# A planner's price for a three-pass matmul: 2.2 columns a nanosecond in place of 2.4

## The chip, the cores and the metric

The kernel runs on one core of one Trainium2 chip. The metric is the device time of one execution in microseconds (us), taken over several runs; a profile of one execution goes with it. The engines are TensorE (PE in the rows, PEld for its weight loads), VectorE (DVE), ScalarE (ACT), GpSimd (POOL) and SyncE (SP), which issues the DMAs.

## The reference

One inference step through two layers of a hybrid backbone, for 128 context tokens and 512 latent tokens that share the weights (float32 throughout). Cut to what is computed in each layer:

```python
mod = SiLU(cond) @ w_mod[l] + b_mod[l]          # shift1, scale1, gate1, shift2, scale2, gate2
h = rms_norm(x) * (1 + scale1) + shift1
proj = h @ w_in[l]     # q | k | v | z | x,B,C of the scan | dt | gate_attn | gate_ssd
attn = softmax(rope(norm(q)) @ rope(norm(k)).T * s) @ v      # 8 query heads, 2 key heads of 128
ssd = norm(ssd_scan(SiLU(dwconv3(x, B, C)), dt, both directions) * SiLU(z))   # chunks of 128
merged = sigmoid(gate_attn) * (attn @ w_attn_o) + sigmoid(gate_ssd) * (ssd @ w_ssd_o)
x = x + gate1 * (merged @ w_out)
h = rms_norm(x) * (1 + scale2) + shift2
u, g = dwconv3(h @ w_up)
x = x + gate2 * ((SiLU(g) * u) @ w_down)
```

Widths: model 1024, inner width of the scan 2048, feed-forward 2816. Keys, values and final scan states of the context tokens are outputs too.

## The kernel before

All 640 tokens, five tiles of 128, pass through each weight once. A float32 product is made of three passes: both operands are split into a high part, which the reduced float32 type `F32R` holds, and a low part, and high x high, low x high and high x low are accumulated in PSUM (`tok_major`, `feat_half`). ScalarE casts a weight block of 128 x 2048 to its high part `wh`, VectorE subtracts to get `wl`. Products with tokens on the partitions have 512 columns and write tiles `pf`; those with features on the partitions (`feat_half`: the convolved inputs of the scan and the up-projection) come in two halves of 386 and 256 columns, also `pf`. Scores of the attention have 320 columns (`pp`), its products with values 512 (`p`), as have the scan's (`p`, `pp`). Transposes and the scan's inner products are plain float32.

Nothing in the program's text is in the order of execution. While the layers are written down, each operation is only recorded, with its engine, a cost in nanoseconds from `_cost`, the earlier operations that it depends on, the buffers that it touches, and a class: `f` for the main stream of projections, `d` for attention and scan, `m` for the modulation of the next layer. Then `issue` plays the whole program through as a list scheduler. It keeps a clock for each of five lanes (TensorE, ScalarE, VectorE, GpSimd, and the one DMA queue), takes again and again the lane that can start something first, and starts on it the ready operation that ranks first:

```python
RANK = {
    "pe": {"m": 0, "d": 1, "f": 2}, "act": {"f": 0, "d": 1, "m": 2}, "dve": {"f": 0, "d": 1, "m": 2},
...
heapq.heappush(avail[e], (self.RANK[e][ops[i][5]], i))
```

So on TensorE an attention or scan operation goes in front of the main stream as soon as the plan says that its operands are there. An operation is ready when its predecessors end, plus a latency from a table `LAT` (160 ns from ScalarE or VectorE to TensorE, 197 ns back), and when a buffer of its kind is free. At the end all operations are issued in the order of their planned starts:

```python
for i in sorted(range(n), key=lambda k: (start[k], k)):
    ops[i][1]()
```

The chip sees only this order: each engine runs its instructions in it and waits where an operand isn't there. VectorE's prices in `_cost` are 70 + 1.04 ns a column (and 60 for each scalar operand), 0.53 ns a column for plain scalings out of SBUF; ScalarE's 52 or 95 + 0.832 ns a column and 93 for each scalar operand. The planner doubles TensorE's prices while it takes its clock for the lower level.

Every operation is recorded by one helper, so all of them have line 178 in the rows, and tiles tell them apart.

Of the kernel before, what the change touches and what calls it, by code (L numbers as in the profile page):

```python
# [79 lines left out]
class Flow:  # L80
# [99 lines left out]
    @staticmethod  # L180
    def _cost(lane, fn, outs, ins, kw):
        def free(ap):
            n = 1
            for d in ap.shape[1:]:
                n *= d
            return n

        n = free(outs[0])
        if lane == "dma":
            return free(outs[0]) * outs[0].shape[0] * 4 / 360.0  # L190
        if lane == "pe":
            if fn == "transpose":
                return 110.0
            if ins[0].dtype == F32R:
                return max(n, 256) / 2.4 + 2 if n > 128 else 213.0
            return max(4 * n / 2.4, 213.0)
        psum = any(a.space == PSUM for a in ins)
        scalars = sum(isinstance(a, bass.AP) for k, a in kw.items() if k in ("scale", "bias", "accum_out"))
        if lane == "act":
            return (52 if psum else 95) + 0.832 * n + 93 * scalars  # L200
        if lane == "pool":
            return 165.0 * n + 300 if ALU.pow in kw.values() else 160.0
        scalars = len(ins) - (2 if fn in ("scalar_tensor_tensor", "tensor_tensor") else 1)
        if fn == "tensor_reduce":
            return 70 + 1.04 * free(ins[0])
        if fn == "reciprocal":
            return 70 + 6.2 * n
        if fn in ("tensor_scalar", "tensor_copy", "memset"):
            return 66 + (1.04 if psum else 0.53) * n + 60 * scalars
        if fn == "scalar_tensor_tensor":  # L210
            return 70 + 1.04 * n + 60 * scalars
        return 70 + 1.04 * n
# [1372 lines left out]
```

## Time and profile before

| | |
|---|---|
| median of 3 runs | 2854.1 us (2854.01 to 2860.25) |
| profiled execution, its own time | 2856.14 us |
| its span in the trace | 2854.3 us |
| TensorE, weight loads | 2816.9 us (99%), 2455.4 us (86%) |
| VectorE, ScalarE, GpSimd | 2067.6 us (72%), 1291.3 us (45%), 90.3 us (3%) |
| data moved | 478.45 MB, 168 GB/s |

The span is the time from the first to the last instruction of the profiled execution. A row of a group gives the engine, the operation, out<-in by tile names, the shape, the count, and then the busy time in us with the mean of one in ns; records of matmuls overlap their neighbours, so a stream's pace is read from starts, not from durations.

### The profile page before, as it was taken

The page shows a single profiled execution, that of the slowest core. Times are in us where ns is not written, and L with a number is a line of the kernel's source. Part 1 is how long each engine was busy: PE and PEld are TensorE (multiplying, and loading weights), DVE is VectorE, ACT ScalarE, POOL GpSimd, SP SyncE. Part 2 cuts the span into 40 slices and gives each one's busy share as a digit, 9 for nine tenths or more (in the row PEclk, how much of TensorE's full clock was granted, in tenths as well). Part 3 has the DMA queues.
Part 4 walks back from the last instruction along what each step waited for, and adds up shares of the span by engine and source line. Part 5 has one row for each costly group of instructions (what it writes and reads, how often), then busy time and mean ns, then how long its engine had stood idle before and what let it go on. Part 6 is the DMA issues. An engine that isn't in the chain of part 4 may idle for free.

```text
span 2854.3 us, 41196 instructions
## 1 busy us (share of the span) xinstructions
PE 2816.9 (99%) x15620; PEld 2455.4 (86%) x15620; DVE 2067.6 (72%) x2851; ACT 1291.3 (45%) x2255; POOL 90.3 (3%) x408
## 2 busy tenths in 40 slices
PE   7999999999999999999999999999999999999999
PEld 4898997788788898998979989878887888989898
DVE  7878775987799599997677666598778456545554
ACT  6454544445353453442444645544454325524342
POOL 1100000000000000000011000000000000000000
PEclk9999999999999999999999999999999999999999
DMA  7344344676768546455352323457667654251523
GB/s 260 104 126 137 114 151 155 209 255 245 276 214 277 177 139 213 164 180 174 104 164 83 95 94 100 151 203 251 221 241 250 205 171 136 86 166 65 157 83 111
DMA packets 309679, 478.45 MB, mean 168 GB/s; under 512 B 19808, under 2 KB 139792, under 8 KB 304360
## 3 DMA queue, kind: packets, MB, share of 16 engines
q1 hardware_dynamic: 309480, 475.81, 49.8%
q8 instruction: 123, 2.02, 0.3%
q14 instruction: 76, 0.62, 0.1%
HBM read 384.08 MB, written 91.65 MB: 167 GB/s over the span
## 4 chain that ended last, share of the span: by engine, by line
PE 94%; DMA 3%; DVE 1%; ACT 1%; issue 0%; SPq 0%; DVEq 0%; ACTq 0%
PE pf L178 79%; PE p L178 10%; PE pp L178 3%; PE pq L178 1%; DMA slab<-in_w_mod_dram 0%; DVE tmp L178 0%; DVE wl L178 0%; DMA tmp<-in_state_ssd_dram 0%; DMA tmp<-sz 0%; DMA mw<-in_w_mod_dram 0%; DMA tmp<-in_x_prompt_dram 0%; DVE slab L178 0%; DMA tmp<-xs 0%; ACT tmp L178 0%; DMA slab<-row 0%
## 5 line engine op out<-in xcount | busy, mean ns | idle before, releaser
L178 PE MATMUL pf<-wh,slab 128*128 128x512 f32 x3920 | 1268.9, 400 | 6.5 <-DVE tmp L178 2.5
L178 PE MATMUL pf<-slab,wh 128*128 128x256 f32 (+1 forms) x4416 | 979.5, 311 | 3.3 <-DVE slab L178 1.9
L178 PEld LDWEIGHTS pf<-wh,slab 128*128 128x128 f32 x3920 | 733.3, 189 | 175.8 <-issue 7.6
L178 PE MATMUL pf<-wl,slab 128*128 128x512 f32 x1960 | 781.5, 399 | 0.2 <-DVE wl L178 0.2
L178 PEld LDWEIGHTS pf<-slab,wh 128*128 128x128 f32 x4416 | 741.1, 188 | 11.9 <-issue 5.5
L178 PE MATMUL pf<-slab,wl 128*128 128x256 f32 (+1 forms) x2208 | 684.5, 310 | 0.0
L178 DVE TENSOR_TENSOR wl<-wr,wh 128x2048 fp32r<-128x2048 f32 (+1 forms) x156 | 350.7, 2248 | 144.4 <-ACT wh L178 143.8
L178 PEld LDWEIGHTS pf<-wl,slab 128*128 128x128 f32 x1960 | 369.6, 189 | 87.1 <-issue 5.8
L178 ACT CAST wh<-wr 128x2048 fp32r<-128x2048 f32 (+1 forms) x156 | 293.0, 1879 | 319.9 <-PE pf L178 302.3
L178 PEld LDWEIGHTS pf<-slab,wl 128*128 128x128 f32 x2208 | 415.6, 188 | 3.1 <-issue 0.2
L178 DVE SCALAR_TENSOR_TENSOR tmp<-tmp,fw,tmp 128x642 f32<-128x642 f32 x176 | 155.5, 885 | 81.0 <-ACT tmp L178 67.0
L178 PE MATMUL p<-tmp,slab 128*128 128x64 f32 (+1 forms) x976 | 209.9, 336 | 1.4 <-DMA tmp<-xs 1.0
L178 ACT ACTIVATE tmp<-tmp 128x642 f32<-128x642 f32 (+2 forms) x176 | 120.9, 687 | 180.1 <-DVE tmp L178 142.3
L178 ACT ACTIVATE tmp<-pf,fw 128x386 f32<-128x386 f32 (+1 forms) x176 | 108.9, 619 | 175.9 <-PE pf L178 172.6
L178 DVE TENSOR_TENSOR tmp<-pf,tmp 128x512 f32<-128x512 f32 x100 | 68.3, 688 | 133.9 <-PE pf L178 133.4
L178 PEld LDWEIGHTS p<-tmp,slab 128*128 128x128 f32 x976 | 136.2, 190 | 17.3 <-ACT tmp L178 4.4
L178 ACT COPY tmp<-pf 128x256 f32<-128x256 f32 (+3 forms) x296 | 127.3, 431 | 43.9 <-PE pf L178 43.8
L178 DVE TENSOR_TENSOR slab<-tmp,slab 128x512 fp32r<-128x512 f32 (+4 forms) x182 | 109.0, 634 | 41.5 <-ACT slab L178 41.3
L178 DVE SCALAR_TENSOR_TENSOR macc<-tmp,cT,macc 128x512 f32<-128x512 f32 x196 | 137.8, 743 | 0.8 <-DMA tmp<-in_w_mod_dram 0.8
L178 DVE TENSOR_TENSOR tmp<-tmp,tmp 128x512 f32<-128x512 f32 (+3 forms) x190 | 133.6, 705 | 5.7 <-DMA tmp<-sz 3.0
L178 ACT ACTIVATE tmp<-pf 128x512 f32<-128x512 f32 (+1 forms) x110 | 63.5, 577 | 141.5 <-PE pf L178 133.6
L178 PEld LDWEIGHTS p<-cst,tmp 128*128 128x128 f32 (+2 forms) x750 | 91.7, 140 | 39.4 <-issue 13.1
(131 smaller groups left out, 2622.1 us busy)
## 6 DMA issues: line engine op xcount, KB each, us to landing
wr<-in_w_in_dram SPq DMA_DIRECT2D x60, 1024.0 KB
wr<-in_w_up_dram SPq DMA_DIRECT2D x44, 1024.0 KB
slab<-row SPq DMA_DIRECT2D x40, 1024.0 KB
tmp<-in_w_mod_dram SPq DMA_DIRECT2D x116, 256.0 KB
tmp<-xres SPq DMA_DIRECT2D x85, 256.0 KB
wr<-in_w_down_dram SPq DMA_DIRECT2D x20, 1024.0 KB
tmp<-xs SPq DMA_DIRECT2D x72, 256.0 KB
xres<-tmp SPq DMA_DIRECT2D x70, 256.0 KB
```

The costliest lines, as they stand in the source:

```text
L178: self.ops.append((lane, lambda: call(*args, **kw), self._cost(lane, fn, outs, ins, kw), deps, touched, self.cls))
```

## The change

One line of `_cost` changes: the planned duration of a three-pass product (operands of type `F32R`) of more than 128 columns. The old one is the columns, at least 256, at 2.4 a nanosecond, plus 2 ns; the new one is the same columns at 2.2 a nanosecond without the 2 ns. Shorter ones keep 213 ns, plain float32 products and transposes keep their prices. The set of instructions, their operands and buffers stay; what the planner makes of them is the order on every engine and in the DMA queue.

```diff
@@ -192,7 +192,7 @@
             if fn == "transpose":
                 return 110.0
             if ins[0].dtype == F32R:
-                return max(n, 256) / 2.4 + 2 if n > 128 else 213.0
+                return max(n, 256) / 2.2 if n > 128 else 213.0
             return max(4 * n / 2.4, 213.0)
         psum = any(a.space == PSUM for a in ins)
         scalars = sum(isinstance(a, bass.AP) for k, a in kw.items() if k in ("scale", "bias", "accum_out"))
```

## Rows read from the trace of the kernel before

**Rows 1.** Page, part 1: busy time, share of the span, instructions.
```profile
PE 2816.9 (99%) x15620; PEld 2455.4 (86%) x15620; DVE 2067.6 (72%) x2851; ACT 1291.3 (45%) x2255; POOL 90.3 (3%) x408
```

**Rows 2.** Page, part 4: the chain that ended last, by engine.
```profile
PE 94%; DMA 3%; DVE 1%; ACT 1%; issue 0%; SPq 0%; DVEq 0%; ACTq 0%
```

**Rows 3.** Windows: stretch, length, busy time by engine, granted clock, DMA share, GB/s.
```profile
0.00:100.00 100.00, 80.19 (x358) 54.59 (x359) 79.71 (x161) 58.79 (x110) 18.73 (x37) 0.97 0.64 219
100.00:2855.00 2755.00, 2736.68 (x15264) 2400.77 (x15262) 1987.89 (x2691) 1232.47 (x2145) 71.55 (x371) 1.00 0.50 166
```

**Rows 4.** TensorE's waits after 100 us: total us, times, longest.
```profile
PE p L178 <- DMA tmp<-in_state_ssd_dram: 2.5, 2, 1.6
PE pp L178 <- DVE tmp L178: 2.1, 1, 2.1
PE pf L178 <- DVE slab L178: 1.9, 2, 1.0
PE pq L178 <- DMA tmp<-modrow: 1.7, 1, 1.7
```

**Rows 5.** Page, part 5: costliest groups of products (count | busy us, mean ns).
```profile
L178 PE MATMUL pf<-wh,slab 128*128 128x512 f32 x3920 | 1268.9, 400 | 6.5 <-DVE tmp L178 2.5
L178 PE MATMUL pf<-slab,wh 128*128 128x256 f32 (+1 forms) x4416 | 979.5, 311 | 3.3 <-DVE slab L178 1.9
...
L178 PE MATMUL pf<-wl,slab 128*128 128x512 f32 x1960 | 781.5, 399 | 0.2 <-DVE wl L178 0.2
...
L178 PE MATMUL pf<-slab,wl 128*128 128x256 f32 (+1 forms) x2208 | 684.5, 310 | 0.0
```

**Rows 6.** Timeline of TensorE: start us, us; first and last of three streams.
```profile
628.16 0.63 PE L178 MATMUL pf<-wh,slab 128*128 128x512 f32 x2
...
633.72 0.63 PE L178 MATMUL pf<-wh,slab 128*128 128x512 f32 x2
...
1001.25 0.39 PE L178 MATMUL pf<-slab,wh 128*128 128x256 f32 x2
...
1011.45 0.39 PE L178 MATMUL pf<-slab,wh 128*128 128x256 f32 x2
...
1011.79 0.52 PE L178 MATMUL pf<-slab,wh 128*128 128x386 f32 x2
...
1015.52 0.52 PE L178 MATMUL pf<-slab,wh 128*128 128x386 f32 x2
```

**Rows 7.** Timeline of VectorE, three instructions back to back.
```profile
1775.47 0.88 DVE L178 SCALAR_TENSOR_TENSOR tmp<-tmp,cw,tmp 128x642 f32<-128x642 f32 x1
1776.27 2.29 DVE L178 TENSOR_TENSOR wl<-wr,wh 128x2048 fp32r<-128x2048 f32 x1
1778.47 0.82 DVE L178 SCALAR_TENSOR_TENSOR tmp<-tmp,tmp 128x642 f32<-128x642 f32 x1
```

**Rows 8.** All waits, those of ScalarE and VectorE for TensorE's `pf`.
```profile
ACT tmp L178 <- PE pf L178: 419.1, 240, 5.8
ACT wh L178 <- PE pf L178: 315.5, 122, 23.5
...
DVE tmp L178 <- PE pf L178: 139.0, 65, 4.2
```

**Rows 9.** Timeline, attention: transposes, VectorE's low part, the product reading it.
```profile
1763.60 0.49 PE L178 MATMUL p<-cst,tmp 128*128 128x128 f32 x3
...
1764.74 0.69 DVE L178 TENSOR_TENSOR tmp<-p,tmp 128x512 fp32r<-128x512 f32 x1
...
1765.76 0.62 PE L178 MATMUL p<-tmp,slab 128*128 128x512 f32 x2
```

**Rows 10.** Timeline, a query/key tile: its last product, last sum, transposes.
```profile
1480.17 0.39 PE L178 MATMUL pf<-wl,slab 128*128 128x512 f32 x1
...
1490.06 0.42 DVE L178 TENSOR_TENSOR tmp<-tmp,tmp 128x256 f32<-128x256 f32 x1
...
1490.67 0.38 PE L178 MATMUL pq<-cst,tmp 128*128 128x128 f32 x2
```

**Rows 11.** Windows in the scan of the first layer (columns as in rows 3).
```profile
700.00:750.00 50.00, 50.00 (x253) 40.70 (x252) 46.81 (x60) 23.50 (x40) 0.00 (x0) 1.00 0.79 275
750.00:800.00 50.00, 48.36 (x223) 38.46 (x223) 36.32 (x54) 22.79 (x45) 0.00 (x0) 1.00 0.83 287
```

## The prediction

> **What bounds the kernel now.** I began with the busy times: TensorE is busy for 2816.9 of 2854.3 us, VectorE for 72% and ScalarE for 45% [rows 1]. The chain that ended last says the same, 94% of it is TensorE [rows 2]. Cut at 100 us, the first stretch holds 19.8 us of TensorE's idle time (100.00 less 80.19) and all the rest only 17.6 us (2754.3 less 2736.68) [rows 3]. Of those 17.6 us the list of waits names small ones: loads of the scan's states 2.5, a VectorE result 2.1, the first up-projection 1.9, a row of the modulation 1.7 [rows 4]. So the span is TensorE's own work, set back to back by the planner, and an order can win at most what is idle. An order can lose more: every instruction that TensorE meets too early in its fixed order makes it wait.
>
> Is a busy TensorE at its limit? The costliest groups are the three-pass products, 5880 of 512 columns and 6624 of 386 or 256 [rows 5]. A record's mean, 400 ns, is no price, since records overlap. Starts are: from 628.16 to 633.72 us stand eight rounds of three 512-column products, so 5.56 us over 24 gives 231.7 ns; seven rounds of 386 columns take 3.73 us, 177.6 ns each; thirty rounds of 256 take 10.20 us, 113.3 ns each [rows 6]. The granted clock there is 1.00 of full speed, the 2.4 GHz level [rows 3], so this is how fast such a stream goes here, whatever the order.
>
> **What the change edits, and what it is worth step by step.** It touches one cost. For 512 columns the planner took 512/2.4+2 = 215.3 ns and will take 232.7; for 386, 162.8 and then 175.5; for 256, 108.7 and then 116.4. Against the measured 231.7, 177.6 and 113.3 [rows 6] the old prices are 7.1, 8.3 and 4.1% short and the new ones within 3%. No instruction is added or removed; each engine's and the DMA queue's order is rewritten. On the groups of [rows 5] the planner's TensorE time grows by 5880 x 17.4 ns = 102 us and 3312 x (12.7 + 7.7) ns = 68 us, 170 us or 6% of the span, since the 6624 are halves of 386 and 256 in equal number. That is planned time, not time on the chip.
>
> Are the other engines' prices right? VectorE's run of three instructions back to back starts at 1775.47, 1776.27 and 1778.47 us [rows 7], 0.80 and 2.20 us apart; by the formulas in the cost function a 642-column multiply-add with a scalar costs 798 ns and a 2048-column subtraction 2200 ns. So before the change only TensorE's three-pass products were priced too short, and VectorE stood relatively 7% too slow in the plan. The plan therefore lets a chain over VectorE and ScalarE last, say, X, puts X/215.3 products between its two ends on TensorE, and these products then take 1.08 X. TensorE comes late to every such chain, and the engines that feed it wait for TensorE instead: ScalarE 419.1 us before evictions and 315.5 us before weight casts, VectorE 139.0 us [rows 8]. After the change the interval holds X/232.7 products, 7.5% fewer, and TensorE arrives when the chain is due. What that costs is 7.5% of each interval less the reserve that the trace shows.
>
> *Short chains.* In the attention loop (2 layers x 2 groups x 4 query tiles x 5 key tiles = 80 of them) the transposes end at 1764.09 (1763.60+0.49), VectorE's low part ends at 1765.43, and the product that reads it starts at 1765.76 [rows 9]. Interval 1.67 us; 7.5% of it is 0.13 us. The reserve is 0.33 us. Part of it is the signal's own way from VectorE to TensorE, at most the 0.19 us that is the smallest reserve shown [rows 10]. 0.33 less 0.19 leaves 0.14, just over 0.13: no wait. I take 0; the bound, if no reserve were there, is 80 x 0.13 = 10 us.
>
> A rule of the Trainium skill speaks against this change: TensorE: Matmul & The Clock Gate, section Back-to-back issue gap, gives the isolated gap at full clock as N/2.4 + 2.5 ns, about 216 ns at 512 columns. The rows of this kernel say 231.7 [rows 6], so rule and trace differ and the measurement decides. If the rule held, the old price would be the right one, there would be no reserve at all, and the estimate for these 80 chains would be the 10 us just named.
>
> *Long chains.* A query or key tile goes from its last product through squares, a reduction, GpSimd's power, the rotation and a final sum to its transposes: from 1480.56 (1480.17+0.39) to 1490.67 us, and the last sum ends at 1490.48, a reserve of 0.19 [rows 10]. 7.5% of 10.1 us is 0.76; if all of the reserve is the signal's way, the whole 0.76 us would be missing. There are 30 such tiles (5 for keys and 10 for queries in each layer). But the interval holds queueing too: the engines in it wait for TensorE in many places [rows 8], and those waits shrink with the interval. I take an eighth of 30 x 0.76 = 23 us, 3 us, since by these rows TensorE is rarely the one that is early; bounds 0 and 23.
>
> *The scan.* Its 40 chunk steps (2 layers x 4 groups x 5) run where VectorE is fullest, 46.81 of 50 us at 700 to 750 us, and in the next slice TensorE already lacks 1.64 us while the DMA engines are at 0.83 [rows 11]. VectorE's work doesn't shrink, and TensorE would come 7.5% sooner. No row gives the length of a chunk's chain; the nearest is the long chain's 0.76 us. Bounds: 0 and 40 x 0.76 = 30 us; I take 3, because VectorE has 13.7 us free in that next slice and the steps can drift into it.
>
> *What may come back.* Waits that VectorE and ScalarE ended sum to a few us in [rows 4], and loads of the scan's states and of the modulation's row to 4.2. With TensorE slower in the plan, the DMA queue's order asks for them earlier in terms of TensorE's work. I take 3 us back of the 17.6; bounds 0 and 17.6. The first 100 us are bound by weights and their casts; I take nothing there.
>
> *Sum.* 0 + 3 + 3 - 3 = +3; with the first up-projection's two waits, which stand on a VectorE chain and grow by about half a microsecond each, +4. The profiled execution took 2856.1 us with a span of 2854.3; the median of the runs shown is 2854.1, so the profiled one is 2.0 above it. 2856.1 + 4 less those 2.0 gives 2858.
>
> **The rivals.** *Slower: the reserve was what kept TensorE fed.* One mechanism: chains that the old order met late by accident are now met on time, and each small lateness becomes a TensorE wait that nobody gives back. Its price is at most 10 + 23 + 30 = 63 us; it counts as slower from 9 us on, that is, once a seventh of this bound is lost. Middle: 20 us, 2874. For it speak the reserves of 0.19 and 0.33 us, which are small [rows 9, 10]; against it that chains shrink as their engines wait less. The skill's gap rule above would put more weight here; the measured 231.7 takes it off.
>
> *Faster: the engines that wait for TensorE pass results on sooner.* A correct plan removes ScalarE's blocking waits of 315.5 us before weight casts, behind which evictions stand in the same queue [rows 8], and with them most of TensorE's 17.6 us: 2854 less 12 is 2842. Against it: these waits end when TensorE's own work ends, so TensorE isn't waiting for their fruit. A second reading would allow much more: the Trainium skill (Trainium Kernel Development and Optimization, Performance Expectations) calls matmul busy time a bad metric and looks at LDWEIGHTS, here 86% [rows 1]. But the start-to-start times of [rows 6] leave no gap that an order could close.
>
> *No effect at all.* The order changes too little to matter: 2854. This lies in the same band as the forecast.
>
> **How the numbers follow.** A measurement here tells a difference from about 0.3%, 8.6 us. Forecast, with no effect: 0.50. Slower rival: 0.31. Faster rival: 0.19. The predicted time is 2858. The range reaches down to the faster rival's 2842 and up to 2880, a little past the slower one's middle; the rest of its bound, up to 2917, is left out. Within the forecast alone I would say 2848 to 2863.
>
> **What the new profile would show.** ScalarE's waits on TensorE before weight casts should fall below half of 315.5 us, and those before evictions fall too: that tests the plan's truth. TensorE's idle time after 100 us should be 18 to 25 us, its waits named after VectorE or ScalarE in the query, key and scan stages rather than after DMAs. Starts of 512-column products stay at 232 ns. I am wrong on the slow side if those waits come to over 27 us, and on the fast side if TensorE's idle time after 100 us falls below 9 us. If TensorE's busy time itself moves by several us, an effect of order on the stream that no row here shows would be at work.

## The result, and the profile after

With 2.2 columns a nanosecond the kernel takes 2892.9 us (median of five, 2885.25 to 2894.07), where the old order takes 2854.1 (median of five, 2851.89 to 2860.25). The recorded ratio is 1.0121, 95% interval 1.0107 to 1.0135; the two medians alone divide to 1.0136. It is slower by four times what a measurement here can tell, and outside the predicted range of 2842 to 2880. The profiled execution took 2892.82 us with a span of 2891.0, 36.7 above the span of before.

Page, part 1, of the kernel after; beside [rows 1] TensorE has the same 15620 instructions and is 16.9 us busier, VectorE and ScalarE are unchanged within 5 us:

```profile
PE 2833.8 (98%) x15620; PEld 2446.2 (85%) x15620; DVE 2062.9 (71%) x2851; ACT 1294.8 (45%) x2255; POOL 86.3 (3%) x408
```

Windows of the kernel after, the stretches of [rows 3] (columns as there):

```profile
0.00:100.00 100.00, 77.66 (x355) 52.08 (x356) 79.26 (x161) 58.63 (x110) 16.15 (x36) 0.98 0.63 218
100.00:2892.00 2792.00, 2756.15 (x15267) 2394.11 (x15265) 1983.65 (x2691) 1236.21 (x2145) 70.19 (x373) 1.00 0.49 164
```

TensorE's idle time after 100 us is 2791.0 (the span of 2891.0 less 100) less 2756.15, 34.9 us, where it was 17.6; before 100 us it is 22.3, where it was 19.8. So the 36.7 us are 19.8 of idle time and 16.9 of busy time.

The waits of TensorE in that second stretch of the kernel after (total us, times, longest). In [rows 4] the longest entry was a load, 2.5 us; now results of VectorE and ScalarE lead:

```profile
PE p L178 <- DVE tmp L178: 11.1, 14, 1.8
PE p L178 <- ACT tmp L178: 9.2, 9, 2.1
PE pp L178 <- DVE tmp L178: 3.0, 3, 1.4
PE pq L178 <- DMA tmp<-modrow: 2.3, 1, 2.3
```

To see where the time went I cut both traces at four places that the program's work marks: the starts of the first 386-column product of the first layer's scan inputs, of its up-projection, and the same two of the second layer. The five stages are then: start; attention, scan and output projections; feed-forward and the next layer's q, k, v; attention and scan again; last feed-forward. Windows of the kernel before, and then of the kernel after:

```profile
0.00:112.80 112.80, 92.99 (x422) 65.15 (x423) 91.90 (x187) 65.31 (x122) 20.16 (x39) 0.97 0.59 199
112.80:978.60 865.80, 860.29 (x4626) 731.86 (x4624) 677.65 (x944) 407.94 (x742) 17.84 (x73) 1.00 0.57 192
978.60:1528.60 550.00, 547.36 (x3194) 496.60 (x3194) 452.02 (x650) 238.21 (x400) 28.60 (x129) 1.00 0.48 158
1528.60:2385.50 856.90, 852.88 (x4594) 729.12 (x4593) 596.53 (x807) 400.97 (x724) 15.03 (x73) 1.00 0.52 177
2385.50:2855.00 469.50, 463.35 (x2788) 432.62 (x2788) 249.50 (x267) 178.82 (x271) 8.64 (x94) 1.00 0.34 109
```

```profile
0.00:115.60 115.60, 93.26 (x433) 64.46 (x434) 94.10 (x191) 65.61 (x122) 18.99 (x39) 0.99 0.57 194
115.60:992.40 876.80, 867.88 (x4615) 729.03 (x4614) 674.29 (x941) 409.78 (x744) 15.74 (x76) 1.00 0.57 190
992.40:1548.80 556.40, 549.56 (x3206) 495.96 (x3205) 453.15 (x651) 240.81 (x400) 26.68 (x127) 1.00 0.47 156
1548.80:2422.20 873.40, 859.77 (x4583) 724.57 (x4582) 591.94 (x805) 399.91 (x724) 14.80 (x75) 1.00 0.52 173
2422.20:2892.00 469.80, 463.33 (x2789) 432.17 (x2787) 249.43 (x265) 178.73 (x269) 10.13 (x92) 1.00 0.34 109
```

The differences are +2.8, +11.0, +6.4 and +16.5 us, and nothing in the last stage (468.8 us from its border to the end of the span in both). The products have the new price there too, but no attention or scan runs beside them. So the loss sits in the stages where TensorE reads from the chains of attention, scan, norms, queries and keys. The counts differ by some ten products of about 0.2 us a stage, so a border is good to some 2 us.

In the second layer's scan the list of TensorE's waits grows from three entries to five. Kernel before (1819.8 to 2385.5 us), and then the same work after (1842 to 2422.2):

```profile
PE pp L178 <- DVE tmp L178: 2.1, 1, 2.1
PE pp L178 <- ACT tmp L178: 0.9, 1, 0.9
PE pf L178 <- DVE wl L178: 0.2, 1, 0.2
```

```profile
PE p L178 <- DVE tmp L178: 5.1, 5, 1.8
PE p L178 <- ACT tmp L178: 2.4, 2, 1.2
PE pp L178 <- DVE tmp L178: 2.2, 2, 1.4
PE p L178 <- DMA tmp<-in_state_ssd_dram: 2.0, 2, 1.1
PE p L178 <- DMA tmp<-xs: 1.7, 1, 1.7
```

3.2 us in 3 waits became 13.4 in 12, none longer than 1.8: many small latenesses, not one big one. One of them in the timeline after:

```profile
2059.34 0.38 SPq L178 DMA_DIRECT2D wr<-in_w_in_dram  x1
...
2059.81 0.60 SPq L178 DMA_DIRECT2D tmp<-xs  x1
...
2062.15 0.69 DVE L178 TENSOR_TENSOR tmp<-tmp,dd 128x512 f32<-128x512 f32 x1 [1.11 <-DMA tmp<-xs]
...
2062.99 1.10 PE L178 MATMUL p<-tmp,slab 128*128 128x512 f32 x2 [1.85 <-DVE tmp L178]
```

The scan's input `xs` is issued right behind a weight load, in the one queue in which both stand; VectorE waits 1.11 us for it, and TensorE 1.85 us for VectorE. SyncE itself waited 839.7 us for VectorE's `wl` over the run after, 766.5 before: a weight load needs the block's buffer, and whatever stands behind it in the queue waits too.

**Where 16.9 us of busy time come from.** The set of products is the same, and a long stream runs as before. Timeline of TensorE after, first and last `wh` product of five rounds of three:

```profile
2548.23 0.63 PE L178 MATMUL pf<-wh,slab 128*128 128x512 f32 x2
...
2551.72 0.64 PE L178 MATMUL pf<-wh,slab 128*128 128x512 f32 x2
```

3.49 us over 15 products is 232.7 ns, as in [rows 6]. What changed is around the reads from chains. Timeline of TensorE after, in the first attention:

```profile
302.98 0.28 PE L178 MATMUL pf<-slab,wh 128*128 128x256 f32 x1
303.20 0.50 PE L178 MATMUL p<-tmp,slab 128*128 128x512 f32 x1
303.54 0.28 PE L178 MATMUL pf<-slab,wh 128*128 128x256 f32 x1
```

The product that reads the chain's `tmp` starts 0.22 us after its predecessor, where 0.11 is the pace, and no idle time is printed, because the predecessor's record lasts 0.28 us. Behind a 512-column product (record 0.40 us, pace 0.23) the first 0.17 us of any wait count as busy. To see whether all of the added busy time is of this kind, I sorted the start-to-start times after 100 us at the full clock, each less the idle time printed in it and less the median of the first product's form. Summed over pairs within the main stream (both write `pf`) this is 36.7 us after and 37.5 before: the stream itself is not slower. Summed over the pairs in which one writes `p`, `pp` or `pq`, products and transposes of the chains, it is 15.9 us more after. So most of the 16.9 us stands at the chains; that it is waiting there is read from examples like the one above.

The lower level of the clock, 1.2 GHz, has a part as well. TensorE's first product behind the longest wait of the first layer's scan, and the window behind it (columns as above):

```profile
769.21 3.68 PE L178 MATMUL p<-tmp,slab 128*128 128x64 f32 x16 [2.10 <-ACT tmp L178]
```

```profile
769.00:776.00 7.00, 6.79 (x24) 6.12 (x25) 4.86 (x6) 2.50 (x7) 0.00 (x0) 0.51 0.71 220
```

The granted clock is 0.51 there, and again 0.57 from 1984 to 1988 us, behind a wait of 1.70 us. After 100 us some 10 us of TensorE's busy time were at the lower level, before the change 3.4; half of each is what it cost, so 3.4 us are added. In the first 100 us the busy time is 2.5 us less than before. 15.9 - 0.8 + 3.4 - 2.5 gives 16.0 of the 16.9.

### The profile page after: what moved, and what is told of

Same layout as the page of the kernel before. It is cut to its first block, busy times and chain, and to the rows that moved or that the text cites. A ratio compares the mean times of both kernels' runs of the same rounds, so it can differ in the third digit from the quotient of the medians.

```text
span 2891.0 us, 41205 instructions
## 1 busy us (share of the span) xinstructions
PE 2833.8 (98%) x15620; PEld 2446.2 (85%) x15620; DVE 2062.9 (71%) x2851; ACT 1294.8 (45%) x2255; POOL 86.3 (3%) x408
## 5 line engine op out<-in xcount | busy, mean ns | idle before, releaser
L178 PE MATMUL p<-tmp,slab 128*128 128x64 f32 (+1 forms) x976 | 215.9, 343 | 10.8 <-DVE tmp L178 6.4
L178 ACT ACTIVATE tmp<-pf,fw 128x256 f32<-128x256 f32 (+1 forms) x176 | 108.9, 619 | 180.1 <-PE pf L178 177.0
L178 DVE TENSOR_TENSOR slab<-tmp,slab 128x512 fp32r<-128x512 f32 (+4 forms) x182 | 108.4, 633 | 38.2 <-ACT slab L178 38.0
L178 PE MATMUL p<-cst,tmp 128*128 128x128 f32 (+2 forms) x750 | 120.2, 276 | 10.4 <-DVE tmp L178 4.7
## 6 DMA issues: line engine op xcount, KB each, us to landing
tmp<-in_w_mod_dram SPq DMA_DIRECT2D x116, 256.0 KB
tmp<-xres SPq DMA_DIRECT2D x85, 256.0 KB
tmp<-xs SPq DMA_DIRECT2D x72, 256.0 KB
xres<-tmp SPq DMA_DIRECT2D x70, 256.0 KB
```

The source lines that it names most:

```text
L178: self.ops.append((lane, lambda: call(*args, **kw), self._cost(lane, fn, outs, ins, kw), deps, touched, self.cls))
```

## The experiments

Three theories were set against each other. **Reserve**: the old price, 4 to 8% below the true pace, made TensorE late to every chain in the plan, and this lateness was what absorbed the errors of the plan; without it each error is a wait. Then a bigger price is worse, and giving the reserve back in another place of the model gets the time back. **Chance**: a list scheduler's order changes everywhere with any small change of its prices, the order of before is a good draw, and any other costs about as much as this one. **Loads**: it is the DMA queue alone that the plan takes too lightly, so only its prices need a reserve. Every ratio below is to the order of before on the same chip.

**The price alone.** One edit, four values:

```diff
-                return max(n, 256) / 2.4 + 2 if n > 128 else 213.0
+                return max(n, 256) / 2.0 if n > 128 else 213.0      # price_20; 2.3, 2.4, 2.6 likewise
```

> Three-pass products priced at 2.0 columns a nanosecond, 256 ns for 512 columns, 10% above the 232 ns that the trace shows; all else as after the change. Lost reserve (the order meets each chain over VectorE and ScalarE with less filler than the old one, and TensorE waits): the loss goes on growing past the true price, 2930 us or more, with TensorE's idle time after 100 us above 60 us. Chance (the order of before is one lucky draw, and any other costs about 1%): some value between 2870 and 2910 without relation to the price. Overfull DMA queue (loads land later than planned; a slower TensorE in the plan asks for them later in terms of TensorE's work): above 2900 too, with waits on loads of the scan's rows above the 43.7 us after the change.

> Priced at 2.3 columns a nanosecond, 222.6 ns for 512 columns, midway between the two versions. Lost reserve and overfull DMA queue: between before and after, 2862 to 2885 us. Chance: 2870 to 2910.

> Priced at 2.4 columns a nanosecond without the 2 ns, 213.3 ns for 512 columns, 1% below before. Lost reserve and overfull DMA queue: as before within 0.3%, 2846 to 2862 us. Chance: another order, so 2870 to 2910.

> Priced at 2.6 columns a nanosecond, 196.9 ns for 512 columns, 9% below before: still more reserve. Lost reserve: no TensorE waits left to remove beyond before's 17.6 us, so 2840 to 2860 us, unless attention and scan now end too late for the products that read them. Chance: 2870 to 2910. Overfull DMA queue: 2840 to 2860.

| price of a 512-column product | median us | ratio (95%) | TensorE idle after 100 us | TensorE busy |
|---|---|---|---|---|
| 2.0: 256.0 ns | 3024.3 | 1.0586 (1.0560 to 1.0612) | 95.7 | 2900.6 |
| 2.2: 232.7 ns (the change) | 2892.9 | 1.0121 (1.0107 to 1.0135) | 34.9 | 2833.8 |
| 2.3: 222.6 ns | 2860.5 | 1.0011 (1.0000 to 1.0022) | 20.1 | 2817.4 |
| 2.4, with the 2 ns: 215.3 ns (before) | 2854.1 | 1 | 17.6 | 2816.9 |
| 2.4 without them: 213.3 ns | 2878.6 | 1.0076 (1.0055 to 1.0097) | 33.5 | 2822.5 |
| 2.6: 196.9 ns | 2938.5 | 1.0288 (1.0262 to 1.0315) | 74.1 | 2837.4 |

The slow side, 2.3, 2.2, 2.0, goes as the reserve theory says, and 5.9% at 2.0 and 0.1% at 2.3 are far from what chance alone should give. But 2.4 without its 2 ns should have been as before and 2.6 harmless, and both are slower. 2878.6 lies in the range of the chance theory; at 2.6 only the exception named in the expectation fits, that attention and scan end too late for the products that read them. At 2.3 the time came out 1.5 us under the 2862 to 2885 expected. At 2.0 ScalarE's and VectorE's waits on the scan's row loads, which the loads theory wanted above 43.7 us, are 43.7, as after the change. The traces show another mechanism on the fast side. Stores of the scan's `y` in the first layer, from 600 us on (duration of the issue in ns, least, median, most; then the first and the last start), before and then at 2.4 without the 2 ns:

```profile
L178 SPq DMA_DIRECT2D y<-tmp x15: 319/320/457, 615.2 to 857.1; - x15
```

```profile
L178 SPq DMA_DIRECT2D y<-tmp x15: 319/319/582, 636.7 to 883.4; - x15
```

The scan ends 26 us later. Behind its end TensorE has nothing left to fill with; timeline at 2.4 without the 2 ns:

```profile
889.71 0.42 SPq L178 DMA_DIRECT2D tmp<-y  x1
...
893.22 0.62 ACT L178 CAST slab<-tmp 128x512 fp32r<-128x512 f32 x1 [8.90 <-DMA tmp<-y]
893.88 0.69 DVE L178 TENSOR_TENSOR slab<-tmp,slab 128x512 fp32r<-128x512 f32 x1 [0.38 <-ACT slab L178]
894.49 0.68 DVE L178 TENSOR_TENSOR tmp<-pf,tmp 128x512 f32<-128x512 f32 x1
...
895.22 1.22 PE L178 MATMUL pf<-wh,slab 128*128 128x512 f32 x2 [8.17 <-DVE tmp L178]
```

The last `y` goes out at 883.4, comes back and is cast; VectorE takes the low part and only then reads a `pf` out, and TensorE's next product has waited 8.17 us for that, the longest wait of the run after its start. Windows around it, at 2.4 without the 2 ns:

```profile
860.00:890.00 30.00, 23.42 (x105) 17.19 (x105) 27.10 (x41) 12.15 (x25) 1.37 (x2) 0.87 0.61 199
890.00:920.00 30.00, 24.22 (x106) 19.28 (x107) 28.74 (x44) 9.12 (x13) 0.00 (x0) 0.84 0.84 287
```

12.4 us of these 60 are idle, and the granted clock is 0.87 and 0.84, so part of the time was at the 1.2 GHz level. These are the two stretches of it:

```profile
861.80:868.60 6.80, 5.42 (x11) 2.56 (x10) 6.80 (x11) 3.42 (x6) 0.00 (x0) 0.50 0.22 77
889.20:899.30 10.10, 3.99 (x11) 2.89 (x12) 9.26 (x15) 0.62 (x1) 0.00 (x0) 0.50 0.79 264
```

TensorE worked 9.4 us in them, half of which, 4.7, the lower level cost; the rest of them was idle anyway. Together 17.1, of the 22.1 that the run lost (2878.59 less 2856.46). At 2.6 it is the same, longer. Window of that run:

```profile
855.00:985.00 130.00, 102.61 (x434) 78.42 (x434) 113.28 (x158) 43.44 (x78) 1.60 (x4) 0.82 0.63 212
```

That window holds 27.4 us of idle time.

The price has two sides. Too long a product, and TensorE meets the chains too early; too short, and the plan puts so many projections into the scan's time that none is left for its end. The products that write `pf` can be counted, from the last `y` store of the first layer to the first up-projection (windows with tile `pf`, TensorE alone; busy time, count): before, after, and at 2.4 without the 2 ns.

```profile
857.10:978.60 121.50, 116.89 (x490) 1.00 0.70 232
```

```profile
827.30:992.40 165.10, 159.94 (x677) 1.00 0.63 212
```

```profile
883.40:1000.80 117.40, 103.22 (x425) 0.96 0.67 221
```

By the code the last projection of the scan's output and the output projection behind it have 480 of them (2 projections x 2 halves x 5 token tiles x 8 x 3 passes); these need the scan's last groups. Before, 490 are left there: the other projections run out just as the scan ends. At 2.4 without the 2 ns 425 are left, at 2.6 420: all else was done by then, and TensorE had to wait. The change is on the other side, with 677, and its last `y` leaves at 827.3 us.

**Giving the reserve back elsewhere.** All keep the price of 2.2. `u_all` makes every other price and latency of the model 8% longer, `u_compute` those of the engines alone, `u_dma` those of the DMA queue alone; `c_104_104` is `u_all` with 4%; `m_pe` lengthens only the latency from ScalarE and VectorE to TensorE.

```diff
-            return free(outs[0]) * outs[0].shape[0] * 4 / 360.0            # u_dma, u_all (c_104_104: 1.04)
+            return free(outs[0]) * outs[0].shape[0] * 4 / 360.0 * 1.08
...
-            return (52 if psum else 95) + 0.832 * n + 93 * scalars         # u_compute, u_all, so on each engine
+            return 1.08 * ((52 if psum else 95) + 0.832 * n + 93 * scalars)
...
-        "act": {"pe": 160.0, "act": 153.0, "dve": 141.0, "pool": 65.0, "dma": 160.0},   # m_pe, "dve" likewise
+        "act": {"pe": 400.0, "act": 153.0, "dve": 141.0, "pool": 65.0, "dma": 160.0},
```

> The new price of 2.2, and every other price of the planner (the other engines' operations, plain float32 products and transposes, all latencies, the DMA queue) raised by 8% too, so that the engines stand to each other nearly as before while TensorE keeps its true price. Lost reserve on the engines' chains, and late DMA alike: as before, 2846 to 2866 us. If a true price of TensorE in itself does harm: near 2893.

> The new price of 2.2; of the others only those of VectorE, ScalarE, GpSimd, plain float32 products, transposes and the latencies between engines raised by 8%, the DMA queue left as it is. Lost reserve on the engines' chains: nearly all comes back, 2850 to 2868 us. Late DMA: little comes back, 2880 us or more.

> The new price of 2.2; of the others only the DMA queue's (set-up, transfer, landing latency) raised by 8%. Lost reserve on the engines' chains: little comes back, 2880 to 2900 us. Late DMA: half or more comes back, 2873 us or less, and ScalarE's waits on the scan's row loads fall from 38.2 towards 18.7 us.

> The new price of 2.2; only the latency from VectorE or ScalarE to TensorE raised from 160 to 400 ns, one 512-column product more in front of every such read. If what is lost is a small lateness at each of TensorE's reads: most comes back, 2855 to 2870 us. If the chains are late by microseconds (queues on VectorE, loads): a fifth at most, 2885 us or more.

> The new price of 2.2, every other price and latency and the DMA queue raised by 4%, half the step of the runs at 8%. Lost reserve: 4% are enough, as at the price of 2.3, so 2854 to 2868 us, with waits on the scan's row loads below 38.2 us. If the true price of TensorE in itself does harm: 2880 or more.

| | median us | ratio (95%) | TensorE idle after 100 us | TensorE busy |
|---|---|---|---|---|
| all prices x1.08 (`u_all`) | 2882.1 | 1.0095 (1.0080 to 1.0110) | 37.6 | 2824.4 |
| engines x1.08 (`u_compute`) | 2866.8 | 1.0041 (1.0026 to 1.0056) | 25.1 | 2822.0 |
| DMA queue x1.08 (`u_dma`) | 2871.7 | 1.0063 (1.0047 to 1.0078) | 20.0 | 2828.6 |
| latency to TensorE 400 ns (`m_pe`) | 2876.1 | 1.0072 (1.0055 to 1.0089) | 23.2 | 2828.9 |
| all prices x1.04 (`c_104_104`) | 2865.4 | 1.0030 (1.0021 to 1.0040) | 22.1 | 2816.5 |

Each is faster than the change itself (`u_all` only just, and with more idle time), and 4% on all prices takes back three quarters of the loss, with TensorE's busy time at before's (its profiled execution stayed at the full clock behind its start, which is worth some 5 us of that). That is the reserve theory's sign. `u_dma` takes back half and `u_compute` two thirds, so their gains overlap, and neither loads alone nor the engines alone are the whole cause. ScalarE's waits on the scan's row loads, 38.2 us after the change, are 25.2 in `u_dma`, as expected, but 37.8 in `u_compute`, which gained more, and 32.8 at the price of 2.3, which lost almost nothing: that row doesn't follow the loss. `m_pe` takes back 40%. TensorE's waits after 100 us in it, beside the first two of the kernel after (11.1 and 9.2):

```profile
PE p L178 <- DVE tmp L178: 4.8, 11, 0.8
PE p L178 <- ACT tmp L178: 3.3, 5, 1.2
```

The longest are 0.8 and 1.2 us, where they were 1.8 and 2.1: a fixed 0.24 us at the read took out long waits too, and idle time fell by 11.7 us, while the time came to lie between the two ranges expected. What `m_pe` and `u_dma` did not get back is for the most part busy time, 12 us above before's in both.

`u_all` missed. It is nearly before's model, scaled, but not quite: 232.7 is 1.081 times 215.3, for 386 and 256 columns the factor is 1.078 and 1.071, the 150 ns that the model takes to free a buffer and its rule for the clock are as they were, and the rest is times 1.08. It should have been as fast, and lost 0.95%. Its scan ends late as at 2.4, the last `y` at 881.1 us, and 413 products are left behind it. So a model that differs by this little can land on the other side, and cost a per cent. That much of the chance theory stands; which of the small differences did it was not tested.

**Where the loss sits.** `scan_new` uses 2.2 only for products recorded with the scan and the output projections, and the old price elsewhere; `scan_old` is its complement.

```diff
+        if not self.scan and lane == "pe" and fn == "matmul" and ins[0].dtype == F32R and ...:   # scan_old: if self.scan
+            cost = cost * 2.2 / 2.4 + 2
```

> The new price holds only for what is recorded with the scan of each layer (the z and gate projections, both output projections, the scan's own products); elsewhere 2.4 columns a nanosecond plus 2 ns as before. If the loss sits stage by stage where chains lost their reserve: the scans' share alone, 4.6 us from the first and 14.5 us from the second, so 2868 to 2880 us, and the stages up to 400 us no longer than before. If the scans pay for what earlier stages leave them: 2862 us or less.

> The complement: the new price everywhere but there. Stage by stage: the rest of the loss, 17.6 us of 36.7 (start 2.8, attention 6.4 and 1.9, feed-forward of the first layer 3.0, keys and queries of the second 3.4), so 2866 to 2880 us. If the scans pay for what earlier stages leave them: above 2880.

`scan_new` takes 2874.7 us, 1.0061 (1.0046 to 1.0076), and `scan_old` 2877.4, 1.0071 (1.0056 to 1.0086). The two sum to 1.32%, the whole change lost 1.21%: half lies with the scan, about 17 us, and half elsewhere, about 20. Both were expected in that size. In the five stages from above, measured against before (us, from the same four starts in each profiled execution):

| | start | attention, scan | feed-forward, next q, k, v | attention, scan | last feed-forward |
|---|---|---|---|---|---|
| the change | 2.8 | 11.0 | 6.4 | 16.5 | 0.0 |
| price 2.0 | 7.7 | 59.1 | 43.5 | 52.2 | 3.8 |
| `scan_new` | -0.5 | 14.6 | -2.0 | 7.7 | -0.7 |
| `scan_old` | 3.8 | 1.8 | 7.9 | 6.9 | 2.5 |
| 2.4 without the 2 ns | 0.5 | 21.7 | -0.4 | 2.5 | -1.3 |
| `u_all` | -1.4 | 21.4 | 2.5 | 5.5 | -0.1 |

The two parts add up to the change's losses stage by stage, 5.4 us off at the most. But `scan_new` was expected to lose 4.6 us in the first scan and 14.5 in the second, and lost 14.6 and 7.7: that the sum fits is luck. The 6.4 us given to the attention in the second expectation were read from a window with 24 more products in it after the change, so most of them were moved work and no loss. With the new price in the scan alone, TensorE's longest lists of waits after 100 us are for VectorE's `tmp`, before `p` 7.6 us in 12 and before `pp` 6.5 in 4, products of the scan; with it everywhere else they are spread over ScalarE's `tmp` 4.2, the up-projection's `slab` 3.8, VectorE's `tmp` 3.2 and the scan's states 3.0. Which step comes late differs from order to order.

**An attempt to beat both.** A price of 2.3 and a latency to TensorE of 240 ns:

> A price of 2.3 and the latency from VectorE or ScalarE to TensorE raised from 160 to 240 ns: a try for a version that beats before. Lost reserve: the waits of TensorE that are left at 2.3 shrink, 2846 to 2862 us. If the order matters by chance within half a per cent: 2850 to 2875.

It takes 2865.5 us, 1.0034 (1.0021 to 1.0047). No order of the twelve is faster than before; that of 2.3 alone can't be told from it, since its interval begins at 1.0000.

## Why the prediction was wrong

The mechanism of the slower rival is what happened, many small latenesses that become waits which nobody gives back; its 31% and its middle of 20 us were too low, and the bound of 63 us held.

- **True pace, price, planned time: right.** The stream runs at 232.7 ns, the new price is the chip's, and TensorE's idle time is named after VectorE and ScalarE. The step that failed is the next one: that a truer plan is met by the chip, so that TensorE arrives when a chain is due and next to nothing is lost (+4 us in the sum). The runs showed 36.7 us in its place. A plan without reserve is missed wherever a chain is late by anything, and TensorE, which is 98% busy, has nowhere to catch up.
- **Busy time: put at nothing.** All terms of the sum are idle time. 16.9 us of the loss are busy time, which the prediction named as a sign of something that no row shows. It is no slower stream: nearly all of it stands around the chains' products, where a short wait prints no idle time, and a part is the lower clock.
- **The scan, "I take 3": failed in size.** `scan_new` measured 0.61%, about 17 us, inside the bounds 0 to 30. The argument that the steps can drift into VectorE's free time left out the order: TensorE stands at the read, and what is free elsewhere doesn't help it.
- **Long chains, "I take an eighth", and the first up-projection, +1: failed in size.** All outside the scan cost 0.71%, about 20 us, for a forecast of 4: in `scan_old` 3.8 in the start, 7.9 in the feed-forward with the next q and k, 8.7 in the two stages that hold attention, 2.5 in the last. "TensorE is rarely the one that is early" was read from waits that don't measure it (below).
- **What may come back, -3: failed.** Idle time after 100 us went from 17.6 to 34.9, the waits for the scan's states and the modulation's row stayed (2.5 and 1.7 us before, 2.2 and 2.3 after), and other loads came later: ScalarE's waits for the scan's `row` went from 18.7 us in 13 to 38.2 in 28, which by itself isn't shown to cost TensorE time.
- **The short chains, 0: not far off.** In the first attention TensorE's printed waits are 0.6 us in the order after, in one, and 0.6 before, in two. The margin, 0.14 us against 0.13, was too thin to show it beforehand, so that part is luck.
- **The test on ScalarE's waits: wrong.** It should have fallen below half of 315.5. All waits after, the rows of [rows 8] and one more:

```profile
ACT tmp L178 <- PE pf L178: 388.9, 225, 6.2
ACT wh L178 <- PE pf L178: 303.5, 123, 23.2
...
ACT tmp L178 <- PE p L178: 176.8, 139, 5.5
DVE tmp L178 <- PE pf L178: 173.0, 66, 4.9
```

The waits before weight casts are 303.5 us. They are waits for a free `wh` buffer of the bound engine, which is always behind; they are no measure of how late TensorE comes to a chain, and at the price of 2.0 they are 351.1. What shrank are those on the chains' own products: for `p` from 228.1 to 176.8 us, in the second layer's scan from 53.5 to 27.8. That looks like the reserve. Over the prices it falls from 262.2 (2.6) and 230.0 (2.4) to 215.0 (2.3) and 176.8, but it is 208.8 at 2.0, the slowest, and 176.0 in `m_pe`, which is faster than the change. So it is a hint and no measure.

- **The skill's rule.** The prediction weighed the slower rival down because the streams measured 231.7 ns against the about 216 of the Trainium skill (TensorE: Matmul & The Clock Gate, section Back-to-back issue gap). The rows settle the pace, 232.7 after the change too, and the section's figure is not what a stream with a weight load each reaches here. But a price near it, 215.3, gives the faster order. The mistake was to let a question of pace decide a question of slack.

**How sure.** Shown: the loss is nothing in the last feed-forward, where no attention or scan runs; it splits over the scan and the rest; a longer price makes it worse in every stage (2.0, 5.9% in all); four ways of giving reserve back clearly recover part of it; on the fast side the scan's end is what is late. Not settled: how much of this one order's 1.2% is the draw, since orders from nearly equal models differed by up to 0.95%, and since before, with 2.3 the fastest of all fourteen orders, may itself be a good draw; why 2 ns of 215 move the scan's end by 26 us, which is some choice in the list scheduling; how loads and engine queues share the scan's part, since their remedies overlap.

## What to carry to other kernels

A static order is a bet that each operand is there when its reader's turn comes, and the engine that bounds the kernel has no time to lose on a lost bet: price that engine a few per cent fast (here the best orders came with products planned 4 and 7% shorter than they are, 2.3 and the old price), or the others slow, and don't expect the truer model to be the better one. Sweep the price on both sides, since too much reserve spends early the work that has to fill a chain's end, and time every order that a small change of the model gives, because neighbours differ by a per cent. Count what is left for the bound engine behind the last chain of a stage: here 490 products were enough and 425 were not. Don't read reserve from the feeding engines' waits for a buffer, and read TensorE's lateness from start to start, since part of it prints as busy time.

## What was not expected of the hardware

Single waits can bring the lower clock. In the kernel after, a wait of 2.10 us was followed by 7 us at 0.51 and one of 1.70 us by 4 us at 0.57; but the longest after 100 us, 2.31, and one of 1.85 were not, so a wait's length alone doesn't tell. Where TensorE starved, at 2.4 without the 2 ns and at 2.6, 17 and 47 us stood at the lower level. Much of that was idle time anyway: TensorE worked 9.4 and 27.8 us in it, so the level cost 4.7 and 13.9 us, on top of 12.4 and 27.4 us of idle time in the same windows. And behind a 512-column product a wait of up to 0.17 us does not show as idle time of TensorE at all, which with the clock is a reason why the same 15620 instructions appear as 2816.5 us of work in one order (`c_104_104`) and 2900.6 in another (`price_20`).
